# Attention's value products as 32-bit products in the array's two column halves, one group a head

## The chip, the cores and the metric

The kernel runs on one core of a Trainium2 chip. The metric is the device time of one execution in microseconds, as the median of several runs. Engines are named as in the profile: PE is TensorE (PEld its weight loads), ACT is ScalarE, DVE is VectorE, POOL is GpSimd, SP is the queue that issues the DMA transfers. PSUM is the memory that TensorE writes, in banks of 512 32-bit numbers on each of 128 partitions; SBUF is the memory from which it reads.

## The reference

One step of a hybrid encoder layer. An input of 1024 prompt frames and 32 frames of a running stream is normalised and projected to queries, keys, values, forget gates and several gate paths. One branch is attention with a forget bias, the other a convolution module; the two are gated, projected, mixed and added to the input. The part that the change touches is the attention of the prompt, 16 heads of 64:

```python
def fox_attend(q, k, v, cq, ck, qpos, kpos):
    s = jnp.einsum('bqhd,bkhd->bhqk', q.astype(jnp.float32), k.astype(jnp.float32))
    bias = jnp.transpose(cq, (0, 2, 1))[:, :, :, None] - jnp.transpose(ck, (0, 2, 1))[:, :, None, :]
    mask = qpos[:, None] >= kpos[None, :]
    s = jnp.where(mask[None, None], s + bias, jnp.finfo(jnp.float32).min)
    p = jax.nn.softmax(s, axis=-1)
    o = jnp.einsum('bhqk,bkhd->bqhd', p, v.astype(jnp.float32))
    return o.astype(v.dtype)
```

## The kernel before

**Halved numbers.** Nearly all products take their operands in the type fp32r, which TensorE works through in one record each, at less than full 32-bit precision. To keep the precision, a number is halved into a high part, rounded to fp32r, and a low part, the difference; a product of two halved numbers is the sum of three products (`mms`, L102: high by high, low by high, high by low). A few places use full 32-bit products instead, with no halving: the running stream's values (L549, four products side by side, each on 32 columns of the array, chosen by the PSUM rows that it writes), the running stream's attention (`Sample`, L870, L871, L906, in the same way), and the layer norm's sums (L1016, over the whole array).

**Stages.** First the input is transposed and the projections run one after another: the gates of the convolution, the values (L592, for 8 tiles of 128 frames by 4 groups of 4 heads), keys and queries. Each value tile leaves PSUM as `vf` (for the output) and as `vb`, which holds for each head 64 high and 64 low columns and goes to DRAM as `s_v`. Then comes the attention stage, from about 600 to 1087 us of the profile, and last the output products (`outproj`).

**Attention.** A head is eight `Block`s of 128 queries; block i sees i+1 tiles of 128 keys. A block goes through three steps, some blocks apart:

- `scores` (L938, L939, L941): products into PSUM (`psS`), the row maximum by DVE (L943), the exponential by ACT (L946), the reciprocal of the sum by DVE, the normalisation of P by POOL (L949).
- `turn`: TensorE transposes P, up to four tiles into one PSUM bank (L966). ACT casts the bank to the high part `pth` (L970), DVE subtracts to get the low part `ptl` (L971). Two blocks share one pair of tiles, 256 queries wide; the corner above the diagonal is cleared by POOL (L956, L957).
- `values`, after every second block: for each key tile, V of the head (128 keys by 64 high and 64 low columns) is the stationary operand and `pth` and then `ptl` the moving one (L982, L983). The upper and the lower 64 rows of the result are the products with V's two parts; ACT copies one (L987), DVE adds the other (L988) into `ot`. For odd heads the pair's result is multiplied by its gate `ga` (L993) and stored as `s_o` (L995).

A head has 2+4+6+8 = 20 key tiles over its four pairs of blocks, so 40 value products of 256 columns.

**Order.** TensorE's order in the attention stage is written out by hand: for block n it issues the scores of block n+3, the transposes of block n, four steps of twelve gate products in all (`fill(4)`, L102, weights of the paths gb, ma and mb) and then the values that are due from block n-2. The other engines and the DMA queue are ordered by a planner that knows the dependences. Banks of `psT`, three in turn, serve transposes and value products; `psS` has two pairs of banks. V has one buffer: the next head's V is loaded once the values of the head's last pair are issued. After the last block two gate tiles follow, while `a_half` loads the stored results and halves them into `ah` and `al` (L1115) for the output products.

Of the kernel before, what the change touches and what calls it, by code (L numbers as in the profile page):

```python
# [8 lines left out]
F32 = mybir.dt.float32  # L9
F32R = mybir.dt.float32r  # L10
# [5 lines left out]
D = 1024  # L16
T = 1024
# [3 lines left out]
H = 16  # L21
# [27 lines left out]
def build(tc, xT, xt, wv, wf, ckT, cv, clT, stT, vec, cst, yT, kT, vO, lfO, cpT, csT):  # L49
    nc = tc.nc  # L50
# [3 lines left out]
    def pool(name, bufs=1, stack=es, **kw):  # L54
        return stack.enter_context(tc.tile_pool(name=name, bufs=bufs, reuse_waits="tile", **kw))

    dram = es.enter_context(tc.tile_pool(name="scr", bufs=1, space=bass.MemoryType.DRAM))
    s_q = dram.tile([2, D, T], F32, name="s_q")
    s_k = dram.tile([2, D, T], F32, name="s_k")
    s_v = dram.tile([8, 128, H, 128], F32, name="s_v")  # L60
    s_vs = dram.tile([TS, D], F32, name="s_vs")
    s_aq = dram.tile([H, 4, T], F32, name="s_aq")
    s_ak = dram.tile([H, 4, T], F32, name="s_ak")
# [1 line left out]
    s_g = {g: dram.tile([8, 128, TT], F32, name=f"s_{g}") for g in ("ma", "mb", "ga", "gb")}  # L65
# [12 lines left out]
    def f32(ap):  # L78
        return ap.bitcast(F32)
# [119 lines left out]
    def pump(n):  # L199
        for _ in range(min(n, len(taps))):  # L200
            taps.pop(0)()
# [49 lines left out]
    def sums(f):  # L251
        return [lambda: from_shift(f, sides["y", f]), lambda: into_sums(f, sides["y", f])]
# [64 lines left out]
    def u_proj(*a, **k):  # L317
        for _ in u_steps(*a, **k):
            pass
# [59 lines left out]
    rows = lambda t: min(128, TT - 128 * t)  # L379
# [89 lines left out]
    scale(0, 1)  # L469
    high(1, 0)  # L470
    low(0, 0, nc.vector)
    steps_of = {}

# [16 lines left out]
    V, G = nc.vector, nc.gpsimd  # L490
# [35 lines left out]
    vp = pool("vp", 2, stack=pvw, side="right")  # L526
# [42 lines left out]
    for c in range(4):  # L569
        if c == 2:  # L570
            pace["rate"] = R_U
            u_proj(2, pj)
            while ("y", 0) not in sides or len(taps) > 62:
                pump(1)

            yr = rounded(sides["y", 0])

            def shifted():
                shift_of(yr)
                taps[:0] = sums(0)  # L580

            later(9, shifted)
        pace["rate"] = R_V
        wh2, wl2 = split.pop(("v", c))
        for t in range(8):
            ps = pj.tile([128, 512], F32, name="pjv", tag="pj")
            n = 0
            for kt in range(KT):
                sl = slice(t * 128, t * 128 + 128)
                wh, wl = wh2[kt // 4][:, kt % 4, :], wl2[kt // 4][:, kt % 4, :]  # L590
                for a, b in ((xh[:, kt, sl], wh), (xl[:, kt, sl], wh), (xh[:, kt, sl], wl)):
                    nc.tensor.matmul(ps[:, :VC], a, b, start=(n == 0), stop=(n == 23))  # L592
# [183 lines left out]
    class Head:  # L776
        def __init__(self, h):
            self.h = h

        def load(self):  # L780
            h = self.h
# [26 lines left out]
    hp = pool("hp", 2, stack=p2, side="right")  # L808
# [23 lines left out]
    psT = pool("psT", 3, stack=p2, space=PS)  # L832
    ap = pool("ap", 2, stack=p2, side="right")
# [86 lines left out]
    class Block:  # L920
# [30 lines left out]
        def turn(self):  # L951
            i, P = self.i, self.P
            if i % 2 == 0:
                tg = f"{(i // 2) % 2}"
                pth, ptl = [ap.tile([128, i + 2, 256], F32R, name=a, tag=a + tg, bufs=1) for a in ("pth", "ptl")]
                nc.gpsimd.memset(f32(pth[:, i + 1, 0:128]), 0.0)  # L956
                nc.gpsimd.memset(f32(ptl[:, i + 1, 0:128]), 0.0)  # L957
                self.head.p = pth, ptl
            self.p = self.head.p
            pth, ptl = self.p  # L960
            qo = slice((i % 2) * 128, (i % 2) * 128 + 128)
            for u in range((i + 4) // 4):
                nj = min(4, i + 1 - 4 * u)
                pt = psT.tile([128, 512], F32, name="ptr2", tag="T")
                for j in range(nj):
                    nc.tensor.transpose(pt[:, 128 * j:128 * j + 128],  # L966
                                        P[:, 128 * (4 * u + j):128 * (4 * u + j) + 128], ident)
                p3 = pt[:, :128 * nj].rearrange("p (j q) -> p j q", j=nj)
                js = slice(4 * u, 4 * u + nj)
                nc.scalar.copy(pth[:, js, qo], p3)  # L970
                nc.vector.tensor_sub(ptl[:, js, qo], p3, f32(pth[:, js, qo]))  # L971

        def values(self):
            if self.i % 2 == 0:
                return
            c, e = self.i // 2, self.head.h % 2
            pth, ptl = self.p
            V, ot = self.head.V, self.head.ot
            njb = 2 * c + 2
            po = psT.tile([128, 512], F32, name="po", tag="T")  # L980
            for j in range(njb):
                nc.tensor.matmul(po[:, :256], V[:, j, :], pth[:, j, :], start=(j == 0), stop=False)  # L982
                nc.tensor.matmul(po[:, :256], V[:, j, :], ptl[:, j, :], start=False, stop=(j == njb - 1))  # L983
# [3 lines left out]
            nc.scalar.copy(ot[own, osl], po[oth, :256])  # L987
            nc.vector.tensor_add(ot[own, osl], ot[own, osl], po[own, :256])  # L988
            if e == 1:
                if c == 0:  # L990
                    self.head.g = ap.tile([128, T], F32, name="ga", tag="kc", bufs=1)
                    nc.sync.dma_start(self.head.g, s_g["ga"][self.head.h // 2, :, :T])
                nc.vector.tensor_mul(ot[:, osl], ot[:, osl], self.head.g[:, osl])  # L993
            if e == 1 and c == 3:
                nc.sync.dma_start(s_o[self.head.h // 2, :, :T], ot)  # L995

    seq = []
# [87 lines left out]
    p3 = ExitStack()  # L1085
# [203 lines left out]
```

## Time and profile before

| | |
|---|---|
| median of 3 runs | 1393.89 us (1393.85 to 1394.35) |
| profiled execution, from first to last instruction (its span, the only time it has here) | 1392.1 us |
| TensorE busy | 1384.3 us, 99% of the span, 9382 products |
| DVE, ACT, POOL busy | 906.5, 642.7 and 623.2 us |
| DMA | 201.24 MB |

Durations of TensorE's products overlap, because each is counted from its start to the end of its results; how far apart two starts are tells what a product holds of the array. A product of full 32-bit operands shows as two records, each with a weight load. "x4" behind a row is a count of records taken together. The chain of work that ended last is followed back from the last instruction, and its shares are shares of the time in question.

### The profile page before, as it was taken

The page shows a single profiled execution, that of the slowest core. Times are in us where ns is not written, and L with a number is a line of the kernel's source. Part 1 is how long each engine was busy: PE and PEld are TensorE (multiplying, and loading weights), DVE is VectorE, ACT ScalarE, POOL GpSimd, SP SyncE. Part 2 cuts the span into 40 slices and gives each one's busy share as a digit, 9 for nine tenths or more (in the row PEclk, how much of TensorE's full clock was granted, in tenths as well). Part 3 has the DMA queues.
Part 4 walks back from the last instruction along what each step waited for, and adds up shares of the span by engine and source line. Part 5 has one row for each costly group of instructions (what it writes and reads, how often), then busy time and mean ns, then how long its engine had stood idle before and what let it go on. Part 6 is the DMA issues. An engine that isn't in the chain of part 4 may idle for free.

```text
span 1392.1 us, 24733 instructions
## 1 busy us (share of the span) xinstructions
PE 1384.3 (99%) x9382; PEld 1346.1 (97%) x9382; DVE 906.5 (65%) x1280; ACT 642.7 (46%) x1318; POOL 623.2 (45%) x669
## 2 busy tenths in 40 slices
PE   8999999999999999999999999999999999999999
PEld 7999999999999999999999999999999999999998
DVE  6687787888898999657766767655555487132111
ACT  6333434646464642245555556655555556222100
POOL 2324254657575875443333444343433257254320
PEclk9999999999999999999999999999999999999999
DMA  5253442424342374344545556454642779444431
GB/s 182 93 179 116 153 136 97 155 85 144 98 164 88 124 207 141 116 124 123 144 137 169 155 147 175 118 152 124 174 134 86 266 265 289 135 150 141 143 107 47
DMA packets 110615, 201.24 MB, mean 145 GB/s; under 512 B 17377, under 2 KB 74593, under 8 KB 110497
## 3 DMA queue, kind: packets, MB, share of 16 engines
q1 hardware_dynamic: 110352, 199.60, 45.7%
q8 instruction: 74, 1.21, 0.4%
q14 instruction: 45, 0.36, 0.1%
q10 hardware_dynamic: 144, 0.07, 0.0%
HBM read 129.78 MB, written 69.84 MB: 143 GB/s over the span
## 4 chain that ended last, share of the span: by engine, by line
PE 97%; DVE 1%; ACT 1%; DMA 0%; issue 0%; POOL 0%; SPq 0%; DVEq 0%; POOLq 0%; ACTq 0%
PE pj L102 71%; PE pjv L592 7%; PE ptr L966 5%; PE po L982 3%; PE po L983 3%; PE psS L938 3%; PE psS L939 2%; PE psS L941 1%; PE pst L716 1%; PE pst L715 1%; PE ptx L434 0%; DMA xtok<-xt 0%; ACT xh L436 0%; PE pjs L549 0%; DVE xl L437 0%
## 5 line engine op out<-in xcount | busy, mean ns | idle before, releaser
L102 PE MATMUL pj<-xh,wh 128*128 128x352 f32 (+2 forms) x1536 | 509.3, 332 | 0.4 <-ACT t L771 0.3
L102 PE MATMUL pj<-xl,wh 128*128 128x352 f32 (+2 forms) x1536 | 494.9, 322 | 0.2 <-DVE xl L437 0.2
L102 PE MATMUL pj<-xh,wl 128*128 128x352 f32 (+2 forms) x1536 | 493.2, 321 | 0.0
L94 POOL TENSOR_TENSOR wl<-raw,wh 128x384 fp32r<-128x384 f32 (+1 forms) x258 | 318.6, 1262 | 234.9 <-ACT wh L91 209.6
L264 DVE SCALAR_TENSOR_TENSOR y<-u,vec_t,y 128x1086 f32<-128x1086 f32 x240 | 378.3, 1577 | 11.5 <-ACT y L261 8.2
L102 PEld LDWEIGHTS pj<-xh,wh 128*128 128x128 f32 x1536 | 289.0, 188 | 3.4 <-issue 0.8
L102 PEld LDWEIGHTS pj<-xl,wh 128*128 128x128 f32 x1536 | 288.7, 188 | 1.4 <-DVE xl L437 1.2
L102 PEld LDWEIGHTS pj<-xh,wl 128*128 128x128 f32 x1536 | 289.4, 188 | 0.2 <-DVE wl L456 0.2
L949 POOL TENSOR_SCALAR P<-P,nm 128x128 f32<-128x128 f32 (+7 forms) x128 | 99.0, 773 | 230.6 <-DVE nm L948 203.1
L943 DVE TENSOR_REDUCE nm<-psS 128x1 f32<-128x128 f32 (+7 forms) x128 | 96.4, 754 | 71.9 <-PE psS L941 70.5
L91 ACT CAST wh<-raw 128x1024 fp32r<-128x1024 f32 x86 | 90.1, 1048 | 112.2 <-PE pj L102 81.0
L970 ACT CAST pth<-ptr 128x512 fp32r<-128x512 f32 (+1 forms) x192 | 89.1, 481 | 81.2 <-PE ptr L966 80.9
L971 DVE TENSOR_TENSOR ptl<-ptr,pth 128x512 fp32r<-128x512 f32 (+1 forms) x192 | 103.3, 550 | 24.0 <-ACT pth L970 22.3
L946 ACT ACTIVATE P<-psS,nm 128x128 f32<-128x128 f32 (+7 forms) x128 | 95.3, 744 | 35.0 <-DVE nm L943 30.3
L733 POOL TENSOR_TENSOR ql<-qn,qh 128x352 fp32r<-128x352 f32 (+1 forms) x48 | 64.6, 1346 | 69.2 <-ACT qh L732 49.8
L966 PE MATMUL ptr<-ident,P 128*128 128x128 f32 x576 | 85.0, 275 | 0.0
L982 PE MATMUL po<-pth,V 128*128 128x256 f32 x320 | 79.0, 283 | 0.0
L983 PE MATMUL po<-ptl,V 128*128 128x256 f32 x320 | 78.6, 281 | 0.0
L592 PE MATMUL pjv<-vwh,xh 128*128 128x260 f32 x256 | 72.5, 283 | 0.0
L592 PE MATMUL pjv<-vwl,xh 128*128 128x260 f32 x256 | 72.5, 283 | 0.0
L592 PE MATMUL pjv<-vwh,xl 128*128 128x260 f32 x256 | 72.3, 283 | 0.0
L938 PE MATMUL psS<-KB,QB 128*128 128x256 f32 (+2 forms) x192 | 67.9, 355 | 0.0
(213 smaller groups left out, 2460.8 us busy)
## 6 DMA issues: line engine op xcount, KB each, us to landing
raw<-wf SPq DMA_DIRECT2D x88, 512.0 KB
s_v<-vb SPq DMA_DIRECT2D x32, 256.0 KB
QB<-s_q SPq DMA_DIRECT2D x32, 256.0 KB
KB<-s_k SPq DMA_DIRECT2D x32, 256.0 KB
V<-s_v SPq DMA_DIRECT2D x16, 512.0 KB
kT<-qn SPq DMA_DIRECT2D x8, 528.0 KB
s_ga<-t SPq DMA_DIRECT2D x24, 176.0 KB
s_gb<-t SPq DMA_DIRECT2D x24, 176.0 KB
```

What stands on the lines that cost most here:

```text
L94: nc.gpsimd.tensor_sub(wl[:, k0:k1, :], raw[:, k0:k1, :], f32(wh[:, k0:k1, :]))
L102: nc.tensor.matmul(ps, a[:, kt, :], b(kt, sl), start=(first and n == 0), stop=(last and n == N - 1))
L264: t = nc.vector.scalar_tensor_tensor(y, u[:, i:i + CW], w, y, op0=ALU.mult, op1=ALU.add)
L592: nc.tensor.matmul(ps[:, :VC], a, b, start=(n == 0), stop=(n == 23))
L938: nc.tensor.matmul(ps[:, b, :wm], QB[:, qsl], KB[:, ksl], start=True, stop=False)
L943: nc.vector.tensor_reduce(nm[:, 0:1], ps[:, :nb, :w], axis=AX.XY, op=ALU.max, negate=True)
L946: nc.scalar.activation(P[:, :nk].rearrange("p (b w) -> p b w", b=nb), ps[:, :nb, :w], AF.Exp, bias=nm[:, 0:1], accum_out=nm[:, 1:2])
L949: nc.gpsimd.tensor_scalar(P[:, :nk], P[:, :nk], nm[:, 2:3], 1.0, op0=ALU.mult, op1=ALU.mult)
L966: nc.tensor.transpose(pt[:, 128 * j:128 * j + 128], P[:, 128 * (4 * u + j):128 * (4 * u + j) + 128], ident)
L971: nc.vector.tensor_sub(ptl[:, js, qo], p3, f32(pth[:, js, qo]))
L982: nc.tensor.matmul(po[:, :256], V[:, j, :], pth[:, j, :], start=(j == 0), stop=False)
L983: nc.tensor.matmul(po[:, :256], V[:, j, :], ptl[:, j, :], start=False, stop=(j == njb - 1))
```

## The change

P is no longer halved: a transposed bank is copied once as plain 32-bit numbers, the first bank of a block by ACT and the second by DVE, into one tile per pair of blocks (`pt0` to `pt3`, of which only the first has two buffers). V is no longer halved either: `s_v` holds 64 columns a head, stored straight from `vf`, and V is 128 keys by 64 columns. The value products of a whole head are issued in one group, when its last pair is due, as full 32-bit products with 64 stationary columns: even key tiles go to the lower 64 rows of PSUM and so to the array's one column half, odd key tiles to the other. That makes 20 products a head in place of 40. Two banks hold the results of all four pairs; ACT copies one half of the rows, DVE adds the other, 512 columns at a time. The gate rows `ga` are asked for when the third pair is due.

```diff
-    s_v = dram.tile([8, 128, H, 128], F32, name="s_v")
+    s_v = dram.tile([8, 128, D], F32, name="s_v")
...
             nc.scalar.copy(vf, ps[:, :256])
-            vb = vp.tile([128, 4, 128], F32R, name="vb", tag="vb", bufs=5)
-            nc.scalar.copy(vb[:, :, 0:64], ps[:, :256].rearrange("p (h d) -> p h d", h=4))
...
-            def low(ps=ps, vb=vb, t=t, c=c):
-                nc.vector.tensor_sub(vb[:, :, 64:128], ps[:, :256].rearrange("p (h d) -> p h d", h=4),
-                                     f32(vb[:, :, 0:64]))
-                nc.sync.dma_start(s_v[t, :, 4 * c:4 * c + 4, :], f32(vb))
-
-            later(3, low)
+            nc.sync.dma_start(s_v[t, :, 256 * c:256 * c + 256], vf)
...
-            self.V = hp.tile([128, 8, 128], F32R, name="V", tag="V", bufs=1)
-            nc.sync.dma_start(f32(self.V), s_v[:, :, h, :].rearrange("b t d -> t b d"))
+            self.V = hp.tile([128, 8, 64], F32, name="V", tag="V", bufs=1)
+            nc.sync.dma_start(self.V, s_v[:, :, 64 * h:64 * h + 64].rearrange("b t d -> t b d"))
...
             if i % 2 == 0:
-                tg = f"{(i // 2) % 2}"
-                pth, ptl = [ap.tile([128, i + 2, 256], F32R, name=a, tag=a + tg, bufs=1) for a in ("pth", "ptl")]
-                nc.gpsimd.memset(f32(pth[:, i + 1, 0:128]), 0.0)
-                nc.gpsimd.memset(f32(ptl[:, i + 1, 0:128]), 0.0)
-                self.head.p = pth, ptl
+                c = i // 2
+                self.head.p[c] = ap.tile([128, i + 2, 256], F32, name="pt", tag=f"pt{c}", bufs=2 if c == 0 else 1)
+                nc.gpsimd.memset(self.head.p[c][:, i + 1, 0:128], 0.0)
...
-                nc.scalar.copy(pth[:, js, qo], p3)
-                nc.vector.tensor_sub(ptl[:, js, qo], p3, f32(pth[:, js, qo]))
+                (nc.vector.tensor_copy if u else nc.scalar.copy)(p[:, 4 * u:4 * u + nj, qo], p3)
 
         def values(self):
-            if self.i % 2 == 0:
+            if self.i == 5 and self.head.h % 2:
+                self.head.g = ap.tile([128, T], F32, name="ga", tag="kc", bufs=1)
+                nc.sync.dma_start(self.head.g, s_g["ga"][self.head.h // 2, :, :T])
+            if self.i < 7:
                 return
...
-            po = psT.tile([128, 512], F32, name="po", tag="T")
-            for j in range(njb):
-                nc.tensor.matmul(po[:, :256], V[:, j, :], pth[:, j, :], start=(j == 0), stop=False)
-                nc.tensor.matmul(po[:, :256], V[:, j, :], ptl[:, j, :], start=False, stop=(j == njb - 1))
-            osl = slice(c * 256, c * 256 + 256)
...
+            pos = [psT.tile([128, 512], F32, name="po", tag="T") for _ in range(2)]
+            for c in range(4):
+                po = pos[c // 2][:, 256 * (c % 2):256 * (c % 2) + 256]
+                for j in range(2 * c + 2):
+                    rows = slice(64 * (j % 2), 64 * (j % 2) + 64)
+                    nc.tensor.matmul(po[rows], V[:, j, :], parts[c][:, j, :], start=(c % 2 == 0 and j < 2),
+                                     stop=(c % 2 == 1 and j >= 2 * c))
+            for u in range(2):
+                sl = slice(512 * u, 512 * u + 512)
+                nc.scalar.copy(ot[own, sl], pos[u][oth])
+                nc.vector.tensor_add(ot[own, sl], ot[own, sl], pos[u][own])
+                if e == 1:
+                    nc.vector.tensor_mul(ot[:, sl], ot[:, sl], self.head.g[:, sl])
```

More of the change, by code (lines that the diff above doesn't have):

```diff
@@ L778, in __init__ @@
             self.h = h
+            self.p = {}
         def load(self):
@@ L953, in turn @@
             if i % 2 == 0:
-                tg = f"{(i // 2) % 2}"
-                pth, ptl = [ap.tile([128, i + 2, 256], F32R, name=a, tag=a + tg, bufs=1) for a in ("pth", "ptl")]
-                nc.gpsimd.memset(f32(pth[:, i + 1, 0:128]), 0.0)
-                nc.gpsimd.memset(f32(ptl[:, i + 1, 0:128]), 0.0)
-                self.head.p = pth, ptl
-            self.p = self.head.p
-            pth, ptl = self.p
+                c = i // 2
+                self.head.p[c] = ap.tile([128, i + 2, 256], F32, name="pt", tag=f"pt{c}", bufs=2 if c == 0 else 1)
+                nc.gpsimd.memset(self.head.p[c][:, i + 1, 0:128], 0.0)
+            p = self.head.p[i // 2]
             qo = slice((i % 2) * 128, (i % 2) * 128 + 128)
@@ L968, in turn @@
                 p3 = pt[:, :128 * nj].rearrange("p (j q) -> p j q", j=nj)
-                js = slice(4 * u, 4 * u + nj)
-                nc.scalar.copy(pth[:, js, qo], p3)
-                nc.vector.tensor_sub(ptl[:, js, qo], p3, f32(pth[:, js, qo]))
+                (nc.vector.tensor_copy if u else nc.scalar.copy)(p[:, 4 * u:4 * u + nj, qo], p3)
         def values(self):
-            if self.i % 2 == 0:
+            if self.i == 5 and self.head.h % 2:
+                self.head.g = ap.tile([128, T], F32, name="ga", tag="kc", bufs=1)
+                nc.sync.dma_start(self.head.g, s_g["ga"][self.head.h // 2, :, :T])
@@ L975, in values @@
+            if self.i < 7:
                 return
[L976 to L979, printed above, removed]
-            po = psT.tile([128, 512], F32, name="po", tag="T")
-            for j in range(njb):
-                nc.tensor.matmul(po[:, :256], V[:, j, :], pth[:, j, :], start=(j == 0), stop=False)
-                nc.tensor.matmul(po[:, :256], V[:, j, :], ptl[:, j, :], start=False, stop=(j == njb - 1))
@@ L984, in values @@
-            osl = slice(c * 256, c * 256 + 256)
+            e, V, ot, parts = self.head.h % 2, self.head.V, self.head.ot, self.head.p
             own = slice(64 * e, 64 * e + 64)
             oth = slice(64 - 64 * e, 128 - 64 * e)
-            nc.scalar.copy(ot[own, osl], po[oth, :256])
-            nc.vector.tensor_add(ot[own, osl], ot[own, osl], po[own, :256])
-            if e == 1:
[L990 to L993, printed above, removed]
@@ L994, in values @@
-            if e == 1 and c == 3:
+            pos = [psT.tile([128, 512], F32, name="po", tag="T") for _ in range(2)]
[5 more added lines that the diff above has]
+                                     stop=(c % 2 == 1 and j >= 2 * c))
```

## The prediction

> **What bounds the kernel now.** I read the page first: busy time by engine, granted clock, and the chain of work that ended last.
>
> ```profile
> span 1392.1 us, 24733 instructions
> PE 1384.3 (99%) x9382; PEld 1346.1 (97%) x9382; DVE 906.5 (65%) x1280; ACT 642.7 (46%) x1318; POOL 623.2 (45%) x669
> ...
> PEclk9999999999999999999999999999999999999999
> ...
> PE 97%; DVE 1%; ACT 1%; DMA 0%; issue 0%; POOL 0%; SPq 0%; DVEq 0%; POOLq 0%; ACTq 0%
> ```
>
> The chain is TensorE nearly throughout, at full clock. What the change saves on VectorE, ScalarE, GpSimd or in DMA is worth nothing by itself; what counts is how long TensorE takes for the values, and whether it is made to wait. The span is 1392.1 us and the runs' median 1393.89, so 1.8 us lie outside the span; the forecast is the median plus the difference of the sum. A difference of about 0.2%, 2.8 us, is what a measurement of this kernel can tell from none.
>
> Second, the same chain cut to the attention stage, 600 to 1100 us, and what TensorE waited for.
>
> ```profile
> by line: PE pj L102 53.2%; PE ptr L966 12.9%; PE po L982 7.6%; PE po L983 7.6%; PE psS L938 7.0%; PE psS L939 6.9%; PE psS L941 1.8%; PE psS L870 0.8%; PE psn L1016 0.7%; PE po L906 0.6%; PE ptr L893 0.3%; issue 0.2%; ACT P L946 0.1%; ACT t
> ```
>
> The two lines of the value products hold 15.2% of 500 us, 76.0 us. Everything else on the chain there is TensorE too; "issue" and ScalarE's exponential hold 0.3%, 1.5 us. So the stage has almost no waiting to win back.
>
> **The value products now.** Third, single products in order of time (start and duration in us, the operands' size, the count).
>
> ```profile
> 844.56 0.28 PE L982 MATMUL po<-pth,V 128*128 128x256 f32 x1
> ...
> 845.86 0.28 PE L983 MATMUL po<-ptl,V 128*128 128x256 f32 x1
> 845.98 0.76 PE L1016 MATMUL psn<-mean,ones_f 128*128 128x352 f32 x2
> 846.30 0.66 PE L938 MATMUL psS<-KB,QB 128*128 128x512 f32 x1
> 846.80 0.39 PE L939 MATMUL psS<-KA,QA 68*128 68x512 f32 x1
> 847.04 0.23 PE L941 MATMUL psS<-cmaskb,identb 128*128 128x128 bf16 x1
> ```
>
> Durations overlap, so the starts are what to read. The third group of a head (6 key tiles, 12 products) runs from 844.56 to 845.98: 0.118 us each. 16 heads have 20 key tiles a head with two products each: 640 x 0.118 = 75.7 us, which agrees with the chain's 76.0. I use 76.0.
>
> **The value products after.** A head has 20 products of full 32-bit operands, 64 rows of output each, alternating between the two column halves. Two rates are needed: what such a product costs, and whether two really run abreast.
>
> The cost: L1016 is a product of 32-bit operands, and the trace shows two records (x2) for each. L939 takes 0.24 us (846.80 to 847.04) and L938, of the same 512 columns, as much, so L1016's two records lasted from 845.98 to 846.56: 0.29 us a record of 352 columns, 0.211 at 256. So one product is two records of some 0.21 us; alone in the array it would cost 0.42 where the halved pair costs 0.24. The change needs both halves at once.
>
> Abreast: the running streams' value projection (L549) has 32-bit products side by side, in column quarters.
>
> ```profile
> 68.31 0.32 PE L102 MATMUL pj<-xl,wh 128*128 128x352 f32 x1
> 68.57 0.43 PE L549 MATMUL pjs<-vraw,xsm 128*32 128x260 f32 x4
> ...
> 68.81 0.62 PE L549 MATMUL pjs<-vraw,xsm 128*32 128x260 f32 x8
> ...
> 69.25 0.40 PE L549 MATMUL pjs<-vraw,xsm 128*32 128x260 f32 x4
> 69.58 0.43 PE L102 MATMUL pj<-xh,wh 128*128 128x352 f32 x1
> 69.86 0.32 PE L102 MATMUL pj<-xh,wl 128*128 128x352 f32 x1
> ```
>
> Sixteen records go in four rounds of four, starting 68.57, 68.81, one between, and 69.25: two rounds in 0.44, so 0.22 us a round of 260 columns, 0.217 at 256. Four abreast cost what one alone costs. Halves are not in the trace; I take two abreast to behave alike, at 0.215 between 0.211 and 0.217. With 1+2+3+4 products a half and two records each, a head has 20 rounds: 4.30 us, 68.8 us for 16 heads.
>
> **The switch.** The same rows show what entering and leaving the divided array costs, which the full-width products did not pay. The product before, L102 at 68.31, would give way after 0.16 us, at 68.47 (L102 products follow each other so at 705.21 and 705.37 below); the first quarter starts at 68.57: 0.10 lost. Its first round takes 0.24 in place of 0.22: 0.02. The last round should end at 69.47; the next product starts at 69.58 (0.11) and holds the array until 69.86, 0.28 in place of 0.16 (0.12). Together 0.35 us. A second group, the sample's values, checks it:
>
> ```profile
> 705.21 0.32 PE L102 MATMUL pj<-xh,wl 128*128 128x352 f32 x1
> 705.37 0.32 PE L102 MATMUL pj<-xl,wh 128*128 128x352 f32 x1
> 705.62 0.66 PE L906 MATMUL po<-vc,pts 128*32 128x64 f32 x32
> 706.09 0.29 PE L906 MATMUL po<-pts 128*32 128x64 f32 x8
> 706.32 0.47 PE L938 MATMUL psS<-KB,QB 128*128 128x448 f32 x1
> 706.63 0.37 PE L939 MATMUL psS<-KA,QA 68*128 68x448 f32 x1
> 706.83 0.36 PE L938 MATMUL psS<-KB,QB 128*128 128x448 f32 x1
> ```
>
> Without a switch L906 would start at 705.53; a score product of 448 columns takes 0.20 (706.63 to 706.83), so the first one, which gave way at 706.63, was served from 706.43 on: 0.90 us for 10 rounds of 64 columns at 0.22 x 64/260 = 0.054, so 0.36 us of switch. The order is the same after the change: gate products, values, scores. A half's first weights are wider:
>
> ```profile
> L549 PEld LDWEIGHTS pjs<-vraw,xsm 128*32 128x32 f32 x64 | 1.7, 109 | 1.4 <-issue 0.4
> L1016 PEld LDWEIGHTS psn<-rstd,ones_f 128*128 128x128 f32 x6 | 1.0, 190 | 0.0
> ```
>
> From 109 to 190 ns over 96 columns is 0.84 ns a column, so the first 64-column load adds 27 ns: 0.38 us a head, bounded by 0.30 and 0.45, 6.1 us for the 16 groups. Sum: 68.8 + 6.1 = 74.9 against 76.0, **1.1 us won**. With both ends: 16 x (4.22 + 0.30) = 72.3 (3.7 won) to 16 x (4.40 + 0.45) = 77.6 (1.6 lost).
>
> One thing could undo this: a load of weights in every round. L906 speaks against it: ten loads of 0.84 x 32 = 27 ns in the open would be 0.27 us and leave 0.09 for its switch, where L549 shows 0.35. The Trainium skill (TensorE: Matmul & The Clock Gate, "Part 3: Packing small matmuls") has a rule that speaks against the change here: a weight load overlaps running products only where the row group differs, and all these products use all rows. By that rule the sum would be that of rival 3 below; the rows just named do not agree with it.
>
> **Waits and the other engines.** Halving the probabilities goes, and these rows show what that was (busy us and mean ns; the 512-wide rows from the attention stage).
>
> ```profile
> L970 ACT CAST pth<-ptr 128x512 fp32r<-128x512 f32 (+1 forms) x192 | 89.1, 481 | 81.2 <-PE ptr L966 80.9
> L971 DVE TENSOR_TENSOR ptl<-ptr,pth 128x512 fp32r<-128x512 f32 (+1 forms) x192 | 103.3, 550 | 24.0 <-ACT pth L970 22.3
> ...
> L971 DVE TENSOR_TENSOR ptl<-ptr,pth 128x512 fp32r<-128x512 f32 x96 | 65.6, 687 | 22.6 <-ACT pth L970 21.3 <-issue 0.4
> L970 ACT CAST pth<-ptr 128x512 fp32r<-128x512 f32 x95 | 55.3, 587 | 56.2 <-PE ptr L966 55.9
> 735.00:852.00 117.00, 117.00 (x863) 109.69 (x862) 78.83 (x158) 67.41 (x158) 46.71 (x82) 1.00 0.54 152
> ```
>
> VectorE loses 103 us of subtractions and gains 64 copies; ScalarE keeps 128 of 192 casts. In the stretch 735 to 852 they were busy 79 and 67 of 117 us beside a TensorE that was never idle, so this buys only part of the 1.5 us of waits: I take 0.4, bounds 0 and 1.5. In the value projection one cast, one subtraction and half the bytes to s_v go; hidden under TensorE, zero. The load of V is halved and is asked for only after the head's one group, with about a head (500/16 = 31 us) to land: zero. On SP's queue the odd heads' gate rows (ga) are asked for later than now, but in the built order still right behind the previous head's V or s_o, ahead of the next head's keys: zero; if they landed late, VectorE's multiplication would hold the row maxima queued behind it.
>
> New waits. Both accumulators take two of psT's three banks at once. After the group ScalarE copies 64 rows of 512 twice (0.59 each by L970), VectorE adds and, for odd heads, multiplies (0.69 each by L971): after the last product 0.59 + 0.69 + 0.69 = 2.0 us until that bank is free. TensorE meanwhile has a block's scores, transposes and 12 gate products (12 x 0.16 = 1.9 us) and then the next block's scores: covered. If the cover went, some 0.4 us a head. On GpSimd the built change puts four clearings of `pt` together behind the previous head's group; the next block's normalisation and weight differences queue behind them. The kernel has such waits already, and GpSimd holds 0% of its chain:
>
> ```profile
> POOL pth L956 <- PE po L982: 40.8, 34, 2.5
> ```
>
> The tail: head 15's result must reach DRAM and come back as the last al before the output products need it.
>
> ```profile
> L102 PE MATMUL pj<-ah,wh x192: 318/325/331, 1109.7 to 1202.7; 128*128 128x352 f32 x192
> L1115 DVE TENSOR_TENSOR al<-a,ah x8: 1246/1259/2071, 1099.9 to 1115.5; 128x1056 fp32r<-128x1056 f32 x8
> ```
>
> The last al ends at 1116.8. It is needed after seven rounds of 9 products from 1109.7: 7 x 9 x 0.16 = 10.1, at 1119.8. Even if all 2.0 us of the evacuation came on top, 1 us of slack would stay: zero; if gone, a microsecond or so, once.
>
> Sum: 1.1 + 0.4 = 1.5 us won, 1393.89 - 1.5 = **1392.4 us**, inside what can be told from no change.
>
> **The rivals.**
> 1. *Switch cheaper, waits gone.* At the lower end of the sum (3.7 won) with most of the 1.5 us of waits gone the result is 1390 or below; midway 1390.7. For it: two halves have less to line up than four quarters. Against: both groups give 0.35. Chance 0.20; faster.
> 2. *Strict order of records.* If a product's two records must follow each other on their half before the other half starts, each group has 21 rounds: 16 x 0.215 = 3.4 us more, 1395.8. Against: L549 starts four records in one round. Chance 0.06; still the same. The Trainium skill (same page and section) has products start in strict program order, which would do this.
> 3. *Weight loads not hidden between rounds* (the other side). A round then costs 0.215 plus 64 x 0.84 = 54 ns: 320 x 0.054 = 17.3 us, 1409.7. It decides from 13 ns a round on (320 x 0.013 = 4.3 us, which turns 1.5 won into 2.8 lost). For it: 64-column loads are twice as long as any the divided array shows; against: L906 hides its loads in rounds of 54 ns, and here there are 215. Chance 0.07; slower.
> 4. *The halves do not overlap*, so the change does not do what it says: 40 rounds a head, 68.8 us more, 1461.2. Against: L549. Chance 0.03; slower.
> 5. *The burst at the head's end holds a bank*: 0.4 us x 16 = 6.4, 1398.8. For it: TensorE has no slack, and blocks without a value group are shorter than before. Against: the cover above. Chance 0.07; slower.
>
> **How the numbers follow.** The forecast has 0.57; its own range by the bounds is 1390.2 to 1395.5. Faster by over 0.2%: rival 1, 0.20. Within 0.2%: forecast and rival 2, 0.63. Slower: rivals 3, 4 and 5, 0.17. The range runs from 1389.5, which holds most of rival 1, to 1399.0, which takes in rivals 2 and 5; rivals 3 and 4 and the ends of 1, under 2 in 10, stay out.
>
> **What would show it.** In the trace after: one group of 40 value records a head, in pairs, from first to last start about 19 x 0.215 = 4.1 us; some 0.1 us before it and a stretched score product behind it; ptl gone and VectorE some 70 us less busy; L102 and the score lines as before. Wrong would be: a pair's rounds over 0.23 us apart (rival 3), 40 separate starts (rival 4), the first half's second record ahead of the other half's first (rival 2), or TensorE waiting on ScalarE or VectorE around L979 and L980 (rival 5).

## The result, and the profile after

The changed kernel takes 1400.35 us (median of 5 runs, 1399.26 to 1401.11) against 1394.35 for the one before in the same series: ratio 1.0042 [1.003, 1.0054], 6.0 us slower. The forecast was 1392.4, with a range that ended at 1399.0. The profiled execution took 1400.09 us, of which 1398.3 are its span.

The page of after: span, busy time, and the chain by engine.

```profile
span 1398.3 us, 24190 instructions
...
PE 1386.1 (99%) x9382; PEld 1313.9 (94%) x9382; DVE 835.5 (60%) x1072; ACT 607.0 (43%) x1190; POOL 635.3 (45%) x605
...
PE 89%; DVE 4%; DMA 3%; ACT 2%; POOL 1%; issue 1%; SPq 0%; ACTq 0%; DVEq 0%; POOLq 0%
```

VectorE and ScalarE have 71 and 36 us less to do, and TensorE is as busy as before (1386.1 against 1384.3). But the chain is now TensorE for 89% where it was 97%: at some places TensorE waits and the chain leaves it. So the span has grown in waits, not in work. The attention stage, to which the whole prediction was given, looks as it should. First the chain cut to 600 to 1100 us, then the order of time around one value group (start and duration in us):

```profile
by line: PE pj L102 50.9%; PE po L975 14.3%; PE ptr L956 12.9%; PE psS L931 7.6%; PE psS L932 7.0%; PE psS L934 1.8%; DMA a<-s_o 1.1%; PE psS L863 0.8%; PE psn L1005 0.8%; PE po L899 0.6%; issue 0.5%; PE ptr L886 0.3%; ACT ah L1103 0.2%; SP
```

```profile
638.05 0.32 PE L102 MATMUL pj<-xh,wl 128*128 128x352 f32 x1
638.20 0.32 PE L102 MATMUL pj<-xl,wh 128*128 128x352 f32 x1
638.46 4.54 PE L975 MATMUL po<-pt,V 128*64 128x256 f32 x40
642.92 0.44 PE L931 MATMUL psS<-KB,QB 128*128 128x384 f32 x1
643.21 0.34 PE L932 MATMUL psS<-KA,QA 68*128 68x384 f32 x1
643.38 0.34 PE L931 MATMUL psS<-KB,QB 128*128 128x384 f32 x1
643.56 0.33 PE L932 MATMUL psS<-KA,QA 68*128 68x384 f32 x1
```

All 40 records of a head stand in one piece. In the trace they start in pairs 6 ns apart, a round each 0.216 us, the first to the last of the 40 in 4.16 us. Around it: the last gate product starts at 638.20 and would give way at 638.36, so 0.10 is lost on entry; the first round takes 0.05 longer; the last record starts at 642.61, so 0.31 pass to the score product where a round takes 0.22; and that score product holds the array for 0.29 (642.92 to 643.21) where the second of its kind takes 0.18. Together 0.35 of switch and 4.67 us a head, 74.7 us for sixteen heads. Read in the same way the groups before the change took 75.8: 1.05 us won.

The loss is seen when each stage of TensorE's work is timed by itself, by the starts of its first and last product in the two traces. In the key and query projections 1.35 us are lost, between them and the first score 0.76, in the first of the three output projections 3.69; the attention stage wins only 0.17 of its 1.05. The start adds 0.26, and the sum is the 5.9 by which the last product is later (0.3 more lie behind it). What TensorE waited for names three of the places (us in total, times, longest; a wait is counted from the end of the product before, so that it comes out smaller than the step between starts):

```profile
PE pj L102 <- POOL wl L94: 2.4, 4, 1.7
...
PE pst L708 <- DVE sql L700: 1.0, 2, 0.5
PE psS L931 <- ACT t L761: 0.6, 1, 0.6
```

Of these only the second was there before, with 0.4. None of the three lies at a line that the change touches.

**The key and query projections.** The chain of waits of after, cut to 320 to 390 us, leaves TensorE at a DMA (start, duration, what):

```profile
323.24 7.88 DMA s_q<-qh
...
331.22 0.49 ACT qh L724
...
333.05 0.50 ACT sqh L697
...
338.58 1.19 DVE sql L700
...
339.82 0.43 PE pst L708
```

A store of the high part of the queries takes 7.88 us; ScalarE can't fill that buffer again until it has landed, and everything behind is late, down to the sums of squares (pst) on TensorE. What crowds the store are loads of the first two heads' queries and keys. SP's queue issues them here, first in the trace before, then in after:

```profile
502.75 0.51 SPq L786 DMA_DIRECT2D QB<-s_q  x1
```

```profile
319.43 0.52 SPq L779 DMA_DIRECT2D QB<-s_q  x1
...
337.84 0.31 SPq L786 DMA_DIRECT2D KA<-s_ak  x1
```

Sixteen loads stand there in the midst of the projections, 180 us ahead of where they were. The addresses of the built kernels tell why: V's tile is half as wide, so the heads' tiles move by 2 KB in each partition (QA begins at byte 190048 in place of 188000) and now lie clear of the projections' last buffer, ql (186848 to 188256). Before, they overlapped, and the loads had to wait for the end of the projections. The first and the sixth experiment test this.

**The first score.** The order of time of after at 600 us:

```profile
600.45 0.46 ACT L761 ACTIVATE t<-pj 128x352 f32<-128x352 f32 x1 [3.35 <-PE pj L102]
...
600.96 0.39 PE L931 MATMUL psS<-KB,QB 128*128 128x256 f32 x1 [0.60 <-ACT t L761]
```

In the built order of banks the last gate tiles ahead of the attention take 2, 4, 0, 3, 1 (before: 2, 1, 0, 3, 4), and the first score tile takes 1 and 2. It has to wait until the very last gate tile is copied out.

**The first output projection.** GpSimd's order of time, before and then after:

```profile
1127.51 3.48 POOL L1132 TENSOR_TENSOR c_l<-y,c_h 128x1056 fp32r<-128x1056 f32 x1
...
1142.23 3.50 POOL L1132 TENSOR_TENSOR c_l<-y,c_h 128x1056 fp32r<-128x1056 f32 x1
1148.03 2.48 POOL L1132 TENSOR_TENSOR c_l<-y,c_h 128x1056 fp32r<-128x1056 f32 x1 [2.30 <-ACT c_h L1131]
1150.47 5.74 POOL L94 TENSOR_TENSOR wl<-raw,wh 128x384 fp32r<-128x384 f32 x3
```

```profile
1142.03 5.75 POOL L94 TENSOR_TENSOR wl<-raw,wh 128x384 fp32r<-128x384 f32 x3
1147.74 3.49 POOL L1121 TENSOR_TENSOR c_l<-y,c_h 128x1056 fp32r<-128x1056 f32 x1
1156.09 2.48 POOL L1121 TENSOR_TENSOR c_l<-y,c_h 128x1056 fp32r<-128x1056 f32 x1 [4.86 <-ACT c_h L1120]
1158.53 5.78 POOL L94 TENSOR_TENSOR wl<-raw,wh 128x384 fp32r<-128x384 f32 x3
```

The same kinds of instructions stand there, but the low parts of the convolution's output (c_l, needed only by the second output projection) lie otherwise against the low parts of the weights (wl): in the built orders GpSimd's pattern is w c c w before, and w c w c c w after. A set of three wl that began at 1150.47 is now queued behind a c_l that waited 4.86 us for ScalarE. It begins at 1158.53, and TensorE waits 1.65 us for its first at 1160.67. ScalarE in turn had stood behind a load. Both, in order of time:

```profile
1154.55 0.50 ACT L1156 ACTIVATE sma<-sma 128x352 f32<-128x352 f32 x1 [6.07 <-DMA sma<-s_ma]
1154.95 1.06 ACT L1120 CAST c_h<-y 128x1056 fp32r<-128x1056 f32 x1
...
1160.67 0.43 PE L102 MATMUL pj<-ah,wl 128*128 128x352 f32 x1 [1.65 <-POOL wl L94]
```

### The profile page after: what moved, and what is told of

It reads as the page before. It is cut to its first block, busy times and chain, and to the rows that moved or that the text cites. A ratio compares the mean times of both kernels' runs of the same rounds, so it can differ in the third digit from the quotient of the medians.

```text
span 1398.3 us, 24190 instructions
## 1 busy us (share of the span) xinstructions
PE 1386.1 (99%) x9382; PEld 1313.9 (94%) x9382; DVE 835.5 (60%) x1072; ACT 607.0 (43%) x1190; POOL 635.3 (45%) x605
## 4 chain that ended last, share of the span: by engine, by line
PE 89%; DVE 4%; DMA 3%; ACT 2%; POOL 1%; issue 1%; SPq 0%; ACTq 0%; DVEq 0%; POOLq 0%
PE pj L102 64%; PE pjv L592 7%; PE po L975 5%; PE ptr L956 5%; PE psS L931 3%; PE psS L932 2%; DMA a<-s_o 1%; PE psS L934 1%; POOL wl L94 1%; DMA s_q<-qh 1%; PE pst L708 1%; DVE y L1112 1%; POOL c_l L1121 1%; DVE y L1113 0%; DVE y L1116 0%
## 5 line engine op out<-in xcount | busy, mean ns | idle before, releaser
L94 POOL TENSOR_TENSOR wl<-raw,wh 128x384 fp32r<-128x384 f32 (+1 forms) x258 | 328.1, 1300 | 242.8 <-ACT wh L91 216.2
L264 DVE SCALAR_TENSOR_TENSOR y<-u,vec_t,y 128x1086 f32<-128x1086 f32 x240 | 383.7, 1599 | 23.4 <-ACT y L261 19.4
L942 POOL TENSOR_SCALAR P<-P,nm 128x128 f32<-128x128 f32 (+7 forms) x128 | 108.6, 849 | 229.4 <-DVE nm L941 197.8
L959 ACT COPY pt<-ptr 128x512 f32<-128x512 f32 (+3 forms) x128 | 65.0, 508 | 102.1 <-PE ptr L956 101.9
L975 PE MATMUL po<-pt,V 128*64 128x256 f32 x640 | 72.6, 382 | 0.0
L941 DVE RECIPROCAL nm<-nm 128x1 f32<-128x1 f32 x128 | 20.7, 162 | 84.3 <-ACT P L939 83.9
L975 PEld LDWEIGHTS po<-pt,V 128*64 128x64 f32 x640 | 44.5, 137 | 24.2 <-issue 3.0
```

The costliest lines, as they stand in the source:

```text
L94: nc.gpsimd.tensor_sub(wl[:, k0:k1, :], raw[:, k0:k1, :], f32(wh[:, k0:k1, :]))
L264: t = nc.vector.scalar_tensor_tensor(y, u[:, i:i + CW], w, y, op0=ALU.mult, op1=ALU.add)
L942: nc.gpsimd.tensor_scalar(P[:, :nk], P[:, :nk], nm[:, 2:3], 1.0, op0=ALU.mult, op1=ALU.mult)
L975: nc.tensor.matmul(po[rows], V[:, j, :], parts[c][:, j, :], start=(c % 2 == 0 and j < 2), stop=(c % 2 == 1 and j >= 2 * c))
```

## The experiments

What each stage of the one profiled execution has more than in the trace before, in us, and the median time of the runs. Medians of the kernel before, run beside them: 1394.47 (1 to 4), 1394.19 (5 to 8), then 1394.62, 1394.44, 1394.45 and 1394.20 (9 to 12).

| kernel | key, query | first score | attention | first output proj. | median | ratio |
|---|---|---|---|---|---|---|
| after | +1.35 | +0.76 | -0.17 | +3.69 | 1400.35 | 1.0042 [1.003, 1.0054] |
| 1 V's tile at its old width | +0.03 | +0.76 | -0.18 | +3.33 | 1398.61 | 1.003 [1.0019, 1.0041] |
| 2 banks in another order | +2.12 | 0.00 | -0.37 | +4.52 | 1399.97 | 1.0039 [1.0025, 1.0052] |
| 3 c_l on VectorE | +1.93 | +0.76 | -0.18 | 0.00 | 1397.28 | 1.0018 [1.0008, 1.0027] |
| 4 all three | +0.03 | 0.00 | -0.33 | 0.00 | 1393.91 | 0.9998 [0.9989, 1.0007] |
| 5 before, c_l on VectorE | +0.01 | 0.00 | +0.02 | 0.00 | 1394.05 | 1.0 [0.999, 1.0009] |
| 6 before, an unused tile | +2.92 | 0.00 | +0.22 | +1.07 | 1396.94 | 1.0018 [1.0008, 1.0028] |
| 7 a group a pair | +2.08 | +0.76 | +13.62 | +1.24 | 1412.61 | 1.0132 [1.0112, 1.0152] |
| 8 one column half | +1.53 | +0.76 | +68.90 | +3.69 | 1468.86 | 1.0535 [1.0514, 1.0556] |
| 9 fourth, gate copies on VectorE | +0.01 | 0.00 | +3.54 | 0.00 | 1397.82 | 1.0025 [1.0016, 1.0034] |
| 10 fourth, group earlier | +0.11 | 0.00 | +0.03 | 0.00 | 1394.06 | 0.9998 [0.9989, 1.0007] |
| 11 tenth, halves swapped | +0.02 | 0.00 | +0.06 | 0.00 | 1394.04 | 0.9998 [0.9989, 1.0007] |
| 12 tenth, a free bank | +0.03 | 0.00 | -1.60 | 0.00 | 1392.44 | 0.9988 [0.9979, 0.9997] |

The profiled executions of 3, 7 and 12 have 0.9 us more in the stage ahead of these, so a column is exacter than a single total. The exception is the first column where the loads come early: the runs of the third kernel spread from 1395.2 to 1398.8 and of the sixth from 1395.1 to 1398.4, where the fifth, with the loads late, spreads from 1393.8 to 1394.9. A step there is one draw of several.

**1, 2, 3 and 4: the three side effects, one by one and together.**

```diff
-            self.V = hp.tile([128, 8, 64], F32, name="V", tag="V", bufs=1)
+            self.V = hp.tile([128, 8, 128], F32, name="V", tag="V", bufs=1)[:, :, 0:64]
```

> The changed kernel, with V's tile as wide as before (128 columns allotted, 64 used), so that the heads' buffers lie where they lay before. Theory (bookkeeping): with the small V the heads' buffers no longer overlap the key and query stage's, so the loads of heads 0 and 1 are issued at 319 us in place of 503 and crowd that stage's stores; the stage (first to last group-sum product) takes 267.4 us in the changed kernel and 266.0 before; here 266.0 again, 1.3 us won there. GpSimd's order in the first output projection comes out differently again, so that stage can move either way by up to 4 us, and the total says little. Rival (the column halves themselves cost the 6 us, the stage differences are scatter of one run): 267.4 stays.

```diff
+    psT = pool("psT", 3, stack=p2, space=PS)
     psS = pool("psS", 2, stack=p2, space=PS)
-    psT = pool("psT", 3, stack=p2, space=PS)
```

> The changed kernel, with the score banks and the transpose banks of PSUM exchanged, so that the first scores do not land in the bank of the last gate tile. Theory: the wait of 0.76 us ahead of the first score product goes: last group-sum product to first score product 109.4 us in place of 110.2; total 1399.6. Rival (column halves cost it): unchanged, 110.2 and 1400.35.

```diff
-        nc.gpsimd.tensor_sub(chl[1][:, f, :], y, f32(chl[0][:, f, :]))
+        nc.vector.tensor_sub(chl[1][:, f, :], y, f32(chl[0][:, f, :]))
```

> The changed kernel, with the convolution branch's low halves (c_l) subtracted on VectorE in place of GpSimd, so that no weight difference (wl) queues behind one. Theory: the 3.7 us lost in the first output projection go: 93.4 us from the first attention output product to the first convolution output product in place of 97.1; total 1396.7. Rival (column halves cost it, or the projection waits for something else): 97.1 and 1400.35.

> The changed kernel with all three edits: V's tile padded, banks exchanged, c_l on VectorE. Theory: 1.3 + 0.8 + 3.7 = 5.8 us won against the changed kernel, 1394.5, within 0.5 of the kernel before; the attention stage stays 0 to 1 us shorter than before. Rival (column halves cost it): 1399 or more.

Each edit makes its own column zero and leaves the other two (which vary: with the loads early the projections lose 1.4 to 2.1). In the second the bank's 0.76 is gone, but those two others grew by 1.6, so that its time alone shows little. Together they bring the kernel back to the time before. So the three places hold the whole loss; what is left to find is why attention wins 0.33 there and not 1.05.

**5 and 6: are these effects of the change, or traps that lay there?**

```diff
+    fp.tile([128, 128], F32, name="pad")
     lf = fp.tile([128, 9, H], F32, name="lf")
```

> The kernel before, with c_l on VectorE as in the third experiment. Theory: before, no weight difference comes late in that stage, so nothing is won: 93.4 us there, total 1394.4 within 0.5. Rival (GpSimd is simply too slow for both, whatever its order): 2 us or more won here too.

> The kernel before, with an unused 512-byte tile that shifts the key and query stage's buffers clear of the heads' buffers, so that heads 0 and 1 are loaded early with no change to attention. Theory: the key and query stage gets about 1.3 us longer, 267.4 in place of 266.0, and the total 1395.7 if the later stages keep their order. Rival (column halves or the lighter value stage cause that stage's loss): 266.0, 1394.4.

c_l on VectorE gains nothing in the kernel before, so the fourth kernel's 6 us are no general improvement. And 512 bytes that nobody uses, put into the kernel before, cost 2.75 us by the medians (1396.94 against 1394.19), with none of the change made. In the profiled execution, one of the longer ones with 1398.10, the loads are early and 2.9 us are lost in the projections, 1.1 in the output projection. So these losses need no change of the value products.

**7 and 8: the prices of the value products.** In the seventh the value group is issued after every second block (64 groups, one bank each); in the eighth all products write the same rows (`rows = oth`), and the addition of the two halves is left out.

> The changed kernel, with the value products issued after every pair of blocks, 64 groups in place of 16, same products. Theory (a group pays 0.37 us for entering and leaving the divided array): 48 x 0.37 = 17.8 us more in the attention stage, total about 1418. Rival (the switch is paid only once the group is long, or hides in the waits): under 5 us more.

> The changed kernel, with all value products on one column half, one after the other (the addition of the two halves is left out, as the sum stands in one). Theory (the two halves run fully abreast in the changed kernel): 40 rounds a head in place of 20, 16 x 20 x 0.216 = 69 us more, total about 1469. Rival (the halves share something, and are no faster than one): 1400.

48 groups more cost 13.8 us in the attention stage (17.8 were expected), 0.29 each, and nearer 0.31, since 1.1 us of the late gate starts told of below are not in this kernel: below the 0.35 read around a group. Four groups are followed directly by the running stream's divided products and five by a transposition, which spares part of the switch. The eighth is the fourth rival made real; its group of the value products, from the busiest groups of instructions (busy us, mean ns), and the one of after:

```profile
L975 PE MATMUL po<-pt,V 128*64 128x256 f32 x640 | 141.6, 380 | 0.0
```

```profile
L975 PE MATMUL po<-pt,V 128*64 128x256 f32 x640 | 72.6, 382 | 0.0
```

The same 640 records of the same length hold the array for twice as long: 217 ns from start to start against 107. A round takes 0.216 us in both: two halves side by side cost what one costs.

**9 to 12: where the attention's own gain went.** In after, nine gate tiles start late behind a transposition, seven by 0.12 to 0.15 us and two by 0.26 (before the change five did, by 0.06 to 0.19). They wait for the one gate bank. The ninth kernel has ScalarE's copies out of that bank on VectorE:

```diff
-                nc.scalar.copy(t, ps)
+                nc.vector.tensor_copy(t, ps)
```

> The changed kernel with the three edits of the fourth experiment (V's tile at its old width, the two pools of banks allotted in the other order, c_l on VectorE), and besides the copies of the gate tiles in the attention stage (t, L763) on VectorE in place of ScalarE. Theory: of the 1.05 us that the value groups win, most is lost again at nine gate tiles whose first product waits about 0.13 us for ScalarE's copy out of the one gate bank, behind a 1024-wide exponential of 1.1 us. Then the late starts go, the attention stage is 0.7 to 1.0 us shorter than in the fourth experiment, about 0.7 to 1.0 us below its 1393.9: 1393.0. Rival: the late starts are the bank's turn as such, and VectorE, whose row maxima are as long, comes late as often: attention within 0.2 us of the fourth experiment, or longer, and 1393.9 or above.

The theory fell: seven of the nine late starts stayed and were later by some 0.08, because VectorE's copy starts 0.03 later and takes 0.50 for ScalarE's 0.45. Two gate tiles waited 1.4 and 0.8 us behind VectorE's other work, and the first gate product behind the last group 1.4, on a bank (below). The copy had not been late at all; what was missing was cover. The order of time in the fourth kernel, and at the same place before the change:

```profile
751.48 0.33 PE L102 MATMUL pj<-xl,wh 128*128 128x352 f32 x1
751.65 0.39 PE L931 MATMUL psS<-KB,QB 128*128 128x512 f32 x1
...
751.85 0.45 ACT L763 COPY t<-pj 128x352 f32<-128x352 f32 x1 [1.19 <-PE pj L102]
...
752.18 0.28 PE L956 MATMUL ptr<-ident,P 128*128 128x128 f32 x1
...
752.35 0.43 PE L102 MATMUL pj<-xh,wh 128*128 128x352 f32 x1
```

```profile
783.09 0.28 PE L983 MATMUL po<-ptl,V 128*128 128x256 f32 x1
783.21 0.39 PE L938 MATMUL psS<-KB,QB 128*128 128x512 f32 x1
783.43 0.39 PE L939 MATMUL psS<-KA,QA 68*128 68x512 f32 x1
783.67 0.23 PE L941 MATMUL psS<-cmaskb,identb 128*128 128x128 bf16 x1
783.73 0.28 PE L966 MATMUL ptr<-ident,P 128*128 128x128 f32 x1
783.77 0.41 PE L102 MATMUL pj<-xh,wh 128*128 128x352 f32 x1
```

ScalarE begins its copy 0.04 after the last product's end and ends at 752.30; the next gate tile starts at once. Between the two gate tiles stand only a score of 512 keys and one transposition. Before the change the head's third pair of value products stood there too, and the gate product followed its transposition by 0.04. Gathering the values into one group took that cover away. So the tenth kernel issues the group behind the transposes of the next head's first block:

```diff
     start(seq[2])
+    done = set()
...
             b.turn()
+            if n and b.i == 0 and pending(seq[n - 1]):
+                seq[n - 1].values()
+                done.add(n - 1)
             fill(4 if b.i > 2 or b.head.h != 8 else 0)
-        if n >= 2 and pending(seq[n - 2]):
+        if n >= 2 and pending(seq[n - 2]) and n - 2 not in done:
             seq[n - 2].values()
```

> The kernel of the fourth experiment (all three edits), and besides a head's value group is issued behind the transposes of the next head's first block, ahead of that block's gate products, instead of one block later. Theory: before the change twelve value products (the head's third pair) stood between the last gate product of one gate tile and the first of the next at a head's end, so that ScalarE's copy out of the one gate bank was covered; gathered into one group they are elsewhere, and only the scores of 512 keys and one transposition, 0.87 us, are left against 0.33 for the end of the products, 0.04, 0.45 for the copy and 0.05: nine starts are 0.13 us late. With the group there again the nine late starts go, and the attention stage is 0.8 us shorter than in the fourth experiment, 1.1 shorter than before the change: 1393.1. Rival: the lateness belongs to the gate tiles as such, or the earlier group waits for the copies of the head's last transposed banks and gives the gain back: attention within 0.3 us of the fourth experiment, 1393.9 or above.

Eight of the nine late starts are gone (two smaller ones are new, 0.09 and 0.04 us), and from the first score to the last value product it takes 1.9 us less than before (0.6 in the fourth). But the time is the fourth's, since one new wait stands at the end:

```profile
1086.01 0.69 DVE L980 TENSOR_TENSOR ot<-ot,po 64x512 f32<-64x512 f32 x1 [1.60 <-ACT ot L979]
...
1086.76 0.43 PE L102 MATMUL pj<-xh,wh 128*128 128x352 f32 x1 [1.40 <-DVE ot L980]
```

The gate product behind the last group takes bank 1, and in this order of banks that is the bank of the group's second half.

> The tenth kernel, and for head 15 alone the two halves of the result change banks, so that the first gate product behind the last value group, which in the tenth waited 1.4 us for VectorE's addition out of the last bank, gets the bank that is free 3 us earlier. Theory: the value groups win 1.05 us and the late gate starts are gone, so with this wait gone too the kernel is 1.3 to 1.6 us below the one before the change, 0.1% (1393.0 against 1394.4), span about 1390.6; from the first score to the last value product 1.9 us less than before the change, as in the tenth. Rival: the wait goes elsewhere (the output products wait for the last head's result instead), and it stays at 1394.0.

The eleventh (`pos.reverse()` for head 15) didn't do what it was to do: the banks were given out in the other order as well, and the second half lay in bank 1 as before. The wait is the same 1.4. The twelfth leaves the group as it is and gives the gate tile another bank:

```diff
+    class FirstPq:
+        n = 0
+
+        def tile(self, *a, **k):
+            self.n += 1
+            return (pq if self.n == 1 else pj3).tile(*a, **k)
+
+    pjG = FirstPq()
...
-        for _ in gate_steps(*fills.pop(0), pj3):
+        for _ in gate_steps(*fills.pop(0), pjG):
```

> The tenth kernel, and the first gate product behind the last value group writes to the gate bank pq, copied out long before, in place of the bank of the last group's second half. In the tenth and the eleventh it waited 1.4 us for VectorE's addition out of that bank; in the eleventh the swap of halves was undone, because the banks are given out in another order too. Theory: that wait goes, the attention stage up to the output products is 1.2 to 1.5 us shorter than before the change (0.3 in the fourth experiment), and the time is 1392.9 against 1394.4 before, ratio 0.999. Rival: something else holds that product or the next tile's first, and the stage stays within 0.3 us of the one before the change: 1394.0.

The wait is gone and the attention stage is 1.60 us shorter than before the change. 1392.44 against 1394.20, ratio 0.9988 [0.9979, 0.9997]: the version that beats both. The gain of 1.8 us is small, but no run of it (1392.28 to 1393.21) reaches one of the kernel before (1393.82 to 1395.79). Its order of time at the place shown above, and its chain by engine:

```profile
752.62 0.28 PE L956 MATMUL ptr<-ident,P 128*128 128x128 f32 x1
752.83 4.54 PE L975 MATMUL po<-pt,V 128*64 128x256 f32 x40
757.29 0.43 PE L102 MATMUL pj<-xh,wh 128*128 128x352 f32 x1
757.56 0.32 PE L102 MATMUL pj<-xh,wl 128*128 128x352 f32 x1
757.72 0.32 PE L102 MATMUL pj<-xl,wh 128*128 128x352 f32 x1
```

```profile
PE 97%; DVE 1%; ACT 1%; DMA 0%; issue 0%; POOL 0%; SPq 0%; DVEq 0%; POOLq 0%; ACTq 0%
```

## Why the prediction was wrong

- **The value products' price: right.** 4.30 us a head was predicted for twenty rounds, 4.32 measured; 0.38 for the switch, 0.35 measured; 74.9 us in all, 74.7 measured. The gain of 1.1 is there, 1.05 as read at one group. The Trainium skill (TensorEngine Tiling (Array Packing), "Key Properties") says that a change of the tiling mode drains TensorE; entering and leaving the divided array cost 0.31 to 0.35 us a group here.
- **Rivals 2, 3 and 4: wrong in the trace.** Rounds of 0.216 with loads of 64 columns leave no place for a load in the open, and starts 6 ns apart none for a strict order of a product's two records. The rule of the Trainium skill that was weighed there (TensorE: Matmul & The Clock Gate, "Part 3: Packing small matmuls": loads overlap running products only where the row group differs) does not hold in these runs: all products use all rows, and their loads (137 ns each) are hidden. The eighth kernel shows that the halves run abreast.
- **"For 1.5 us of waits I take 0.4 won": the wrong sign.** The group's place, priced at nothing, cost 0.8: gate starts behind a transposition are late by 1.59 us in all in the fourth kernel, by 0.76 before (each counted beyond the usual 0.028). The prediction named the cover of the value banks and did not ask what the value products themselves had been covering. With 1.05 won and 0.83 lost, 0.22 of the fourth kernel's 0.33 is accounted for; at most 0.1 is left for what VectorE and ScalarE were relieved of. With the group elsewhere (twelfth) attention wins 1.60, of which 0.4 come from late starts that are then fewer than before the change (0.36).
- **"The load of V is halved ... zero", the value projection "zero" and GpSimd's order: the steps that failed.** They were costed by their own work, which is indeed nothing. What cost 5.8 us is what they moved: a tile of another size shifted addresses (1.35), the gate tiles came into other banks (0.76), and GpSimd's queue came out in another order some 50 us after the last touched instruction (3.69). For the loads the sixth kernel shows that the good placement before was luck; for the banks and GpSimd's order that was not tried. Nothing in the sum or the range stood for any of the three, though all three stand in the built kernel (its addresses, banks and orders), which the prediction read for the attention stage alone.
- **Rival 5 (a bank held at the head's end)**: not in after; its mechanism appeared once, at the last head of the ninth to eleventh kernels, with 1.4 us in place of 0.4 a head.
- **The tail: right.** The last al ended at 1117.8, and the output products did not wait for it. VectorE goes on from it to the convolution's output (y at 1117.73 in place of 1116.63 before). That is 1.1 us later from the span's start, but the first output product starts 2.2 us later by then, from the losses ahead of it; counted from that product, y starts 5.8 us behind it in place of 6.9. So a late result of the last head does not explain the longer output projection.

Open: why the early loads cost 1.35 us in one kernel and 2.9 in another, or whether that is only the spread between executions; which part of the change moved the banks; and what moved c_l against wl. There the built order and the load that ScalarE waited for were not told apart, since the third experiment takes c_l out of that queue altogether. The first late gate start (0.13 us late, at 623 us) stayed in the twelfth.

## What to carry to other kernels

Full 32-bit products that fill half the columns run two abreast at the price of one (0.216 us a key tile here, where the halved pair took 0.236), so they can replace halved products at about equal cost, if groups are long enough to pay some 0.3 us of switch each. In a kernel whose chain is 97% one engine, ask of each edit what it moves: addresses that made a load wait, the rotation of banks, a planner's queue, and above all what the moved work was covering. Such effects were over five times the direct one here, and are found by timing stage by stage, not by looking where the edit was made.

## What was not expected of the hardware

The price of leaving the divided array shows in the product behind the group, and it is the same for a score product and a gate product. A score product behind the group holds the array 0.11 us longer (642.92 to 643.21 against 643.38 to 643.56), and so does a gate product in the twelfth kernel (757.29 to 757.56 against 757.56 to 757.72). So moving the group did not make its switch cheaper; its place decides only which starts it covers. A transposition behind a group pays less: in the seventh kernel 0.06 us (1095.31 to 1095.47 against 1095.47 to 1095.58). Why it does was not tried.
